# Two layers of an encoder on one core: the output projection as seven block products, and the first gate and up columns together

## The chip, the core and the metric

The kernel runs on one core of a Trainium2 chip. A core has a matrix engine (TensorE, in the profile PE, with its weight loads as PEld), a vector engine (VectorE, DVE), a scalar engine (ScalarE, ACT), GpSimd (POOL), and queues that issue transfers: SP's (SyncE), GpSimd's and ScalarE's. Matrix products land in PSUM, which is used here as eight banks of 512 columns of fp32. Everything else works in SBUF, with 128 partitions. An engine takes its own instructions strictly in the order in which the program wrote them, and waits on semaphores for the others.

The metric is the device time of one execution in microseconds, the median of several runs.

## The reference, cut to what matters

The input is 512 tokens of width 1024, in fp32, and there are two layers. One layer is:

```
h = rms_norm(x, attn_norm_g[l])
z = einsum('bsd,dc->bsc', h, w_in[l])          # q, k, v of two attention branches, and the gates ga, gb
ya = einsum('bsc,cd->bsd', window_gqa(...), w_proj_a[l])
yb = einsum('bsc,cd->bsd', neighbourhood_attn(...), w_proj_b[l])
mixed = sigmoid(ga) * ya + sigmoid(gb) * yb
x = x + einsum('bsd,de->bse', mixed, w_out[l])             # w_out is 1024 x 1024
h = rms_norm(x, ffn_norm_g[l])
u = silu(einsum(h, w_gate[l])) * einsum(h, w_up[l])        # 1024 x 2816 each
x = x + einsum('bsf,fd->bsd', u, w_down[l])                # 2816 x 1024
```

## The kernel before, in words

**Arithmetic.** Activations lie transposed, as eight tiles `xT[k]` of 128 channels by 512 tokens. A product keeps fp32 accuracy by splitting both operands into a high part and the rest: each pair of 128 x 128 weights and 128-row activations costs three matrix products (high by high, high by rest, rest by high). The high part is a ScalarE copy into a rounded type, the rest a VectorE subtraction. For some weights the rest is made another way: ScalarE writes the negated high part and a transfer on GpSimd's queue adds the raw weights to it in SBUF (`low_by_transfer`, `w_low`).

**Seven products.** The feed-forward part (columns 256 and up, in five "quads" of 512 columns) already uses a seven-product scheme: a 2 x 2 split of weights and activations into blocks, seven products of sums of blocks in place of eight. `Quad` loads the four weight blocks and makes their sums and parts; `chain_x` makes the seven activation operands (four sums, seven high parts, seven rests of 128 x 1024 elements each) from the normalised `xn`; `m_step` issues one product, 24 instructions with 256 columns, and evacuates it. The order of the products is `ORDER = (1, 5, 6, 2, 7, 3, 4)`. Four of them share banks. Product 1 goes to bank a; ScalarE copies a into bank b (`seed`). Product 5 goes to bank d and ScalarE fetches it into SBUF. Product 6 adds onto b; VectorE then writes b plus the fetched 5 into a third bank c (`seed_c`, through `plus`). Product 2 adds onto a, product 7 adds onto b, 3 onto c, 4 onto b again.

**The stage of this document.** After the two attention projections (`evac_a`, `evac_b`) come, in each layer:
- the output projection w_out: four column pairs in `pair_matmul`, each 8 x 2 x 3 = 48 products with 512 columns, 192 in all. Each of the eight mixed tiles gets its high part and rest in `chain_m`. `evac_x` adds each result tile to `xT[k]`, and `nrm.chunk` makes the parts of the next norm's operand and the running sum of squares; in layer 0 each tile is also written away to DRAM for later.
- the norm: `Norm.chain` sums the squares over partitions with a tiny product against `ones`, VectorE takes the reciprocal square root of the four columns in 15 tiny instructions, TensorE turns it into rows, VectorE copies the rows to SBUF.
- the first 256 columns of w_gate and then of w_up, as two column pairs (48 products with 512 columns each), `evac_g` and `evac_u`; the norm's row factor is applied only at these evacuations, so that the products may start before the norm is known.
- the quads, which need the normalised `xn`, hence the rows: four scaled VectorE instructions for each half of the channels.
In layer 1, `chain_out` also turns x back to token order with 32 small TensorE products (eight groups of four) and ScalarE copies.

**What sets the order.** The Python code writes one stream of instructions for each engine. A main generator issues the products; side chains (`spawn`) are served in the order of a list and advance when a table of estimated engine times says that their inputs are there (`Need`; with `backlog=XLOG` a chain may run up to 6 us ahead into VectorE's queue). Evacuations (`soon`) and weight preparation (`at_pos`) are tied to positions of the product stream. All buffers lie in two SBUF arenas and eight banks, packed by first and last use. All instructions go through one helper, line 346, so that the profile knows them by tile, operation and shape only.

## Time and profile before

| what | value |
|---|---|
| runs | 1356.54, 1358.61, 1358.91 us; median 1358.61 us |
| the profiled execution | 1358.36 us, of which the span of the profile is 1356.6 us |
| granted clock of TensorE | 1.000 |
| instructions in the span | 21344 |
| ScalarE, GpSimd busy | 844.9 us (62%), 301.5 us (22%) |
| read from and written to HBM | 174.63 MB, 4.19 MB |
| transfers from SBUF to SBUF on GpSimd's queue | 94 |

The profiled execution took 1.8 us more than its span, so a microsecond in the trace is a microsecond of the metric. Page lines give busy time and share; where engines are shown by stage, the columns are the stretch, its length, and for each engine the busy time in it and the number of instructions. Matrix products overlap in the pipeline, so that the mean duration of one is longer than the distance to the next; what counts is the distance from start to start.

### The profile page before, as it was taken

What the parts mean: (1) busy time and instruction counts of PE and PEld (TensorE: products, weight loads), DVE (VectorE), ACT (ScalarE), POOL (GpSimd) and SP (SyncE); (2) the same over time, 40 slices, a digit from 0 to 9 for tenths busy, and PEclk for the clock granted to TensorE, in tenths of its full rate; (3) what the DMA queues carried; (4) which work ended last, traced back from release to release, by engine and by line L of the source; (5) the groups of instructions that cost most, each with busy time, mean ns of one, the idle gap of its engine ahead of it and who ended that gap; (6) DMA issues with size and microseconds to landing.
All of it is one profiled execution on the core that took longest, in us unless ns stands there. A gap on an engine that the chain in (4) does not pass through costs nothing.

```text
span 1356.6 us, 21344 instructions
## 1 busy us (share of the span) xinstructions
PE 1348.2 (99%) x7980; PEld 1195.8 (88%) x7980; DVE 1013.2 (75%) x1856; ACT 844.9 (62%) x1322; POOL 301.5 (22%) x323
## 2 busy tenths in 40 slices
PE   9999999999999999999999999999999999999998
PEld 7888888888899999999888888888888999999997
DVE  6876878455857787878968667784559587878888
ACT  6577677544666657667455676675447656667572
POOL 5542222310211101011243423223002111011110
PEclk9999999999999999999999999999999999999999
DMA  9997888876887778587979978889649867695873
GB/s 224 197 168 137 161 155 150 161 173 202 173 189 188 171 181 202 148 212 192 224 150 197 153 147 149 161 151 185 171 109 168 218 143 171 172 248 123 222 180 98
DMA packets 194279, 234.76 MB, mean 173 GB/s; under 512 B 26992, under 2 KB 156448, under 8 KB 194176
## 3 DMA queue, kind: packets, MB, share of 16 engines
q0 software_dynamic: 102656, 143.64, 56.2%
q1 hardware_dynamic: 91024, 89.08, 22.1%
q8 instruction: 63, 1.03, 0.3%
q10 hardware_dynamic: 496, 0.67, 0.2%
q14 instruction: 40, 0.33, 0.1%
HBM read 174.63 MB, written 4.19 MB: 132 GB/s over the span
## 4 chain that ended last, share of the span: by engine, by line
PE 90%; DVE 4%; ACT 3%; issue 2%; DMA 1%; POOL 0%; SPq 0%; ACTq 0%; POOLq 0%
PE banks L346 90%; DVE arena L346 4%; ACT arena L346 3%; DMA arena<-in_w_in 1%; DMA arena<-in_x 0%; POOL arena L346 0%; ACT sm L346 0%; SPq L346 0%; DVE banks L346 0%; DVE sm L346 0%; DVE den L346 0%; DVE negm L346 0%; ACTq L346 0%; POOLq L346 0%
## 5 line engine op out<-in xcount | busy, mean ns | idle before, releaser
L346 PE MATMUL banks<-arena 128*128 128x512 f32 (+1 forms) x7406 | 1313.6, 337 | 1.6 <-DVE arena L346 0.8
L346 PEld LDWEIGHTS banks<-arena 128*128 128x128 f32 x7406 | 1130.9, 190 | 142.8 <-DVE arena L346 2.2
L346 ACT CAST arena<-arena 128x1024 fp32r<-128x1024 f32 (+2 forms) x377 | 321.2, 882 | 183.8 <-DVE arena L346 172.8
L346 DVE TENSOR_TENSOR arena<-arena,arena 128x1024 fp32r<-128x1024 f32 (+2 forms) x284 | 267.0, 950 | 35.8 <-ACT arena L346 34.0
L346 ACT ACTIVATE arena<-arena 128x1024 fp32r<-128x1024 f32 (+2 forms) x292 | 252.3, 885 | 40.4 <-DMA arena<-in_w_in 19.0
L346 POOL DMA_DIRECT2D arena<-in_w_in x163 | 162.3, 1388 | 313.0 <-ACT arena L346 285.4
L346 DVE TENSOR_TENSOR arena<-arena,banks 128x512 f32<-128x512 f32 (+1 forms) x205 | 138.3, 682 | 121.4 <-PE banks L346 121.3
L346 DVE TENSOR_TENSOR arena<-arena 128x1024 f32<-128x1024 f32 (+4 forms) x256 | 220.7, 875 | 4.5 <-DMA arena<-in_w_gate 2.1
L346 DVE TENSOR_TENSOR arena<-banks,arena 128x512 f32<-128x512 f32 (+4 forms) x230 | 152.8, 669 | 61.4 <-PE banks L346 34.0
L346 POOL DMA_DIRECT2D arena<-arena x94 | 84.2, 896 | 496.7 <-ACT arena L346 335.8
L346 ACT COPY arena<-banks 128x512 f32<-128x512 f32 (+1 forms) x106 | 61.6, 585 | 74.1 <-PE banks L346 72.8
L346 ACT CAST arena<-banks 128x512 fp32r<-128x512 f32 (+2 forms) x116 | 64.4, 555 | 63.8 <-PE banks L346 62.5
L346 ACT ACTIVATE arena<-arena,negm 128x256 f32<-128x256 f32 (+1 forms) x128 | 68.2, 533 | 18.8 <-DVE negm L346 16.9
L346 PE MATMUL banks<-cst,arena 128*128 128x128 f32 x504 | 77.0, 275 | 2.3 <-DMA arena<-in_x 1.0
L346 PEld LDWEIGHTS banks<-cst,arena 128*128 128x128 f32 x504 | 61.6, 141 | 12.3 <-DVE arena L346 1.5
L346 DVE CUSTOM_DVE_ANT_0 arena<-banks,cst,nsnk 128x256 f32<-128x256 f32 (+1 forms) x64 | 34.5, 548 | 33.8 <-PE banks L346 33.1
L346 DVE CUSTOM_DVE_ANT_0 arena<-banks,arena 128x256 f32<-128x256 f32 x64 | 26.4, 420 | 21.5 <-PE banks L346 21.2
L346 ACT ACTIVATE arena<-arena,vec2T 128x512 fp32r<-128x512 f32 x16 | 11.6, 727 | 47.4 <-DVE arena L346 47.4
L346 ACT ACTIVATE arena<-banks 128x512 f32<-128x512 f32 x30 | 18.0, 598 | 35.4 <-PE banks L346 35.3
L346 POOL DMA_DIRECT2D arena<-in_w_up x8 | 8.3, 1035 | 122.7 <-PE banks L346 80.3
L346 DVE TENSOR_SCALAR arena<-arena,sm 128x256 f32<-128x256 f32 (+1 forms) x88 | 29.4, 385 | 1.1
L346 POOL DMA_DIRECT2D arena<-in_w_proj_b x16 | 17.5, 1287 | 52.5 <-ACT arena L346 52.5
(69 smaller groups left out, 366.7 us busy)
## 6 DMA issues: line engine op xcount, KB each, us to landing
arena<-in_w_in POOLq DMA_DIRECT2D x99, 512.0 KB, 7.2
arena<-arena POOLq DMA_DIRECT2D x94, 512.0 KB, 6.8
arena<-in_w_up SPq DMA_DIRECT2D x40, 512.0 KB
arena<-in_w_down SPq DMA_DIRECT2D x40, 512.0 KB
arena<-in_w_gate SPq DMA_DIRECT2D x36, 512.0 KB
arena<-in_w_in POOLq DMA_DIRECT2D x64, 256.0 KB, 6.8
arena<-in_w_proj_a POOLq DMA_DIRECT2D x16, 512.0 KB, 7.4
arena<-in_w_proj_b POOLq DMA_DIRECT2D x16, 512.0 KB, 7.5
```

The source lines that it names most:

```text
L346: f(*args, **kw)
```

## The change

It has four parts.

1. **w_out as two quads.** `plan_out` makes two `Quad`s for each layer, for the output columns 0 to 511 and 512 to 1023, with the loads and sums due 6 and 3 us earlier than the position alone would give. The mixed activations are collected in two tiles `mt` of four channel groups; `chain_seven` (the former `chain_x`, made general, with the high part of operand 5 now made before the rest of operand 1) makes their seven operands. `block_step` (the former `m_step`, made general) issues the products in the order q0: 1, 5; q1: 1, 5; q0: 6, 2, 7, 3, 4; q1: 6, 2, 7, 3, 4. Each finished block is added to a pair of channel tiles `xp` by `add_x`; when both token halves of a pair are there, its two norm chunks are spawned as chains (`gchunk`), and in layer 0 the pair is written away, four transfers of twice the size in place of eight.
2. **Gate and up together.** The first 256 columns of w_gate and w_up use four banks at once: channel tiles 0 to 3 for gate, then for up, then tiles 4 and 5 for all four column tiles, then 6 and 7. Evacuations become chains.
3. **Token order in layer 1.** The change to token-by-column order that layer 1 needs is now made where the gates and projections are evacuated (`into`, `out_of`) and by eight ScalarE copies of x (`chain_turn`) ahead of w_out.
4. **Chain order.** The operands of the first quad go to the head of the list of chains; `chain_out` waits for the up columns to be evacuated; the end of layer 0 (`chain_end`) is put at the head of the list and may run ahead into VectorE's queue.

The core of the diff:

```diff
+    OUT_EARLY = (6.0, 3.0)
...
+    OUT_STEPS = [(q, m) for q in range(2) for m in ORDER[:2]] + [(q, m) for q in range(2) for m in ORDER[2:]]
+
+    def plan_out(l):
+        w = a["w_out"][l]
+        for q in range(2):
+            srcs = [w[512 * h : 512 * h + 512, 512 * q : 512 * q + 512] for h in range(2)]
+            quads[l, q, "w_out"] = Quad(srcs, 0.0, False)
+        for q, m in OUT_STEPS:
+            quads[l, q, "w_out"].due(m, total[0] - OUT_EARLY[q])
+            total[0] += 24 * 0.12
...
     def plan_ffn(l):
-        plan_pair(a["w_gate"][l], 0, KD, on_engines=True)
-        plan_pair(a["w_up"][l], 0, KD)
+        for k0 in range(0, KD, 4):
+            plan_pair(a["w_gate"][l], 0, 4, P * k0, on_engines=True)
+            plan_pair(a["w_up"][l], 0, 4, P * k0)
...
+            yield from begin(0)
+            b11, b12 = tiles[0][:, :, :256], tiles[0][:, :, 256:]
             n1, n2 = buf([4, 256]), buf([4, 256])
-            yield from normal(0)
             yield from high(1, b11)
             V.tensor_tensor(n1, b11, b12, ALU.subtract)
+            yield from high(5, n1)
             yield from low(1)
-            yield from high(5, n1)
             yield from low(5)
-            yield from normal(1)
+            yield from begin(1)
...
+            soon({
+                1: seed,
+                5: fetch,
+                6: seed_c,
+                2: lambda: quadrant(0, 0, o, 1.0),
+                7: lambda: quadrant(1, 1, plus(act()), -1.0),
+                3: lambda: quadrant(0, 1, o, 1.0),
+                4: lambda: quadrant(1, 0, o, -1.0),
+            }[m])
...
+        def add_x(q, i, t, src, sign):
+            at = 2 * q + i
+            x = xp[at][:, :, 256 * t : 256 * t + 256]
+            op = ALU.add if sign > 0 else ALU.subtract
+            V.tensor_tensor(x, x, src.rearrange("p (j n) -> p j n", j=2), op)
+            blocks_of[at] += 1
+            if blocks_of[at] == 2:
+                for j in range(2):
+                    spawn(nrm.gchunk(2 * at + j))
+                if l < DEPTH - 1:
+                    soon(lambda: Q.dma_start(away[at], xp[at]), 1.0)
+
+        for q, m in OUT_STEPS:
+            yield f"m{l}{m}"
+            yield from block_step(quads[l, q, "w_out"], m, ms[m], lambda *x, q=q: add_x(q, *x))
...
+        lead = [mm_bank(), mm_bank(), at_bank(), at_bank()]
+        for k0 in range(0, KD, 4):
+            wk = [w_take(), w_take()]
+            for k1 in range(k0, k0 + 4, 4 if k0 == 0 else 2):
+                for n, o in enumerate(lead):
...
```

How the streams move is seen in three places of layer 0. First TensorE, from the projections to the first quad: the products with 512 columns from the last gates on, the sum of squares against `ones`, the turn of the norm into rows (`rstd`), and the first products with 256 columns of the first quad. Before:

```order
L346 MATMUL banks<-arena_72 128x512 x420
L346 MATMUL banks<-ones,arena_71 128x1 x4
L346 MATMUL banks<-arena_72 128x512 x18
L346 MATMUL banks<-cst,rstd_3112 128x128 x4
L346 MATMUL banks<-arena_72 128x512 x60
L346 MATMUL banks<-arena_72 128x256 x144
```

The same place on TensorE in the change:

```order
L346 MATMUL banks<-arena_72 128x512 x210
L346 MATMUL banks<-arena_72 128x256 x336
L346 MATMUL banks<-arena_72 128x512 x45
L346 MATMUL banks<-ones,arena_71 128x1 x4
L346 MATMUL banks<-arena_72 128x512 x18
L346 MATMUL banks<-cst,rstd_3321 128x128 x4
L346 MATMUL banks<-arena_72 128x512 x33
L346 MATMUL banks<-arena_72 128x256 x144
```

The 192 products of w_out became 336 with half the columns. The product against `ones` stood 18 products behind the end of w_out (the 420 are 210 for what comes before, 192 for w_out and 18 of the 96 for gate and up) and now stands 45 behind it; from the rows to the first quad there were 60 products and there are now 33.

Second VectorE, from the copy of the norm's rows to the second half of the normalised activations (the second `x4`; the 1024-element instruction behind it is the operand of product 6). Before:

```order
L346 COPY arena_71<-banks 128x512
L346 SCALAR_TENSOR_TENSOR arena_71<-arena_71,vec2T 128x512 x4
L346 TENSOR_TENSOR arena_72<-arena_71,arena_72 128x1024
L346 TENSOR_TENSOR arena_71<-banks,arena_71 128x512 x2
L346 TENSOR_TENSOR arena_71<-arena_71 128x1024
L346 TENSOR_TENSOR arena_71<-arena_71 128x4x256
L346 TENSOR_TENSOR arena_72<-arena_71,arena_72 128x1024
L346 TENSOR_TENSOR arena_71<-banks,arena_71 128x512
L346 TENSOR_TENSOR arena_71<-arena_71 128x512
L346 TENSOR_TENSOR arena_72<-arena_71,arena_72 128x1024
L346 SCALAR_TENSOR_TENSOR arena_71<-arena_71,vec2T 128x512 x4
L346 SCALAR_TENSOR_TENSOR arena_71<-arena_71 128x1024
```

The same place on VectorE in the change:

```order
L346 COPY arena_71<-banks 128x512
L346 SCALAR_TENSOR_TENSOR arena_71<-arena_71,vec2T 128x512 x4
L346 TENSOR_TENSOR arena_71<-arena_71 128x1024
L346 TENSOR_TENSOR arena_71<-arena_71 128x4x256
L346 TENSOR_TENSOR arena_72<-arena_71,arena_72 128x1024 x2
L346 SCALAR_TENSOR_TENSOR arena_71<-arena_71,vec2T 128x512 x4
L346 SCALAR_TENSOR_TENSOR arena_71<-arena_71 128x1024
```

The evacuations of gate and up (the rows that read banks) moved out of this stretch to behind it, and the two scaled halves moved together.

Third VectorE, directly behind, up to the instruction that writes a bank from a bank: that is `seed_c`, which reads bank b between products 6 and 7. Before:

```order
L346 SCALAR_TENSOR_TENSOR arena_71<-arena_71 128x1024
L346 TENSOR_TENSOR arena_71<-banks,arena_71 128x512
L346 TENSOR_TENSOR arena_72<-arena_71,arena_72 128x512
L346 TENSOR_TENSOR arena_72<-arena_71,arena_72 128x1024 x2
L346 TENSOR_TENSOR arena_71<-arena_71 128x4x256
L346 TENSOR_TENSOR arena_71<-arena_71 128x512
L346 TENSOR_TENSOR banks<-banks,arena_71 128x512
```

And in the change:

```order
L346 SCALAR_TENSOR_TENSOR arena_71<-arena_71 128x1024
L346 TENSOR_TENSOR arena_71<-banks,arena_71 128x512 x2
L346 TENSOR_TENSOR arena_72<-arena_71,arena_72 128x1024 x2
L346 TENSOR_TENSOR arena_71<-arena_71 128x4x256
L346 TENSOR_TENSOR arena_71<-banks,arena_71 128x512
L346 TENSOR_TENSOR arena_71<-arena_71 128x512
L346 TENSOR_TENSOR arena_72<-arena_71,arena_72 128x1024 x2
L346 SCALAR_TENSOR_TENSOR arena_71<-arena_71 128x1024
L346 TENSOR_TENSOR banks<-banks,arena_71 128x512
```

Between the operand of product 6 and the read of bank b stood six instructions, three of them with 1024 elements, and there now stand ten, six of them with 1024 elements; added are the rests of operands 7 and 3 and the sum for operand 4, and the evacuations of the gate columns. The rest of operand 6 is the first of the first pair.

More of the change, by code (lines that the diff above doesn't have):

```diff
@@ L776, in trunk @@
             plan_pair(a["w_proj_b"][l], 256 * c, 4)
-        for c in range(4):
-            plan_pair(a["w_out"][l], 256 * c, KD, on_engines=True)
+        plan_out(l)
         plan_ffn(l)
@@ L1632, in layer @@
-        last = l == DEPTH - 1
-        A.activation(warm, ones, AF.Silu)
-        spawn(nrm.chain())
-        xo = []
-        def chain_out():
-            yield Need(keys=["x_out", f"rows{nrm.i}"])
-            for b in range(NB):
-                xo.append([act() for _ in range(2)])
-                for half in range(2):
-                    part = xT[4 * half : 4 * half + 4]
-                    yield Need("pe", part, [at_slots])
-                    at_slots.take()
-                    ps = at_bank()
-                    for i in range(4):
-                        T.transpose(ps[:, P * i : P * i + P], part[i][:, P * b : P * b + P], ident)
-                    yield Need("act", [ps])
-                    A.copy(xo[b][half], ps)
-                    at_slots.give(clock["act"])
-            done.add("xo")
@@ L1655, in layer, with chain_seven @@
[L1655 to L1667 removed]
+        def chain_seven(tag, parts, tiles, begin):
@@ new lines, in layer, with chain_out @@
+        for q, m in OUT_STEPS:
+            yield f"m{l}{m}"
+            yield from block_step(quads[l, q, "w_out"], m, ms[m], lambda *x, q=q: add_x(q, *x))
+        last = l == DEPTH - 1
+        A.activation(warm, ones, AF.Silu)
+        spawn(nrm.chain())
+        xo = []
+        def chain_out():
+            yield Need(keys=["x_out", f"rows{nrm.i}", f"{key}up0", f"{key}up1"])
+            for b in range(NB):
+                xo.append([act() for _ in range(2)])
+                for half in range(2):
+                    part = xT[4 * half : 4 * half + 4]
+                    yield Need("pe", part, [end_slots])
+                    end_slots.take()
+                    ps = at_bank()
+                    for i in range(4):
+                        T.transpose(ps[:, P * i : P * i + P], part[i][:, P * b : P * b + P], ident)
+                    yield Need("act", [ps])
+                    A.copy(xo[b][half], ps)
+                    end_slots.give(clock["act"])
+            done.add("xo")
```

281 lines of the change are left out of this document (136 added, 145 removed).

## The prediction

> **What bounds the kernel now.** I read the page's busy times and its chain of waits first.
>
> ```profile
> span 1356.6 us, 21344 instructions
> ...
> PE 1348.2 (99%) x7980; PEld 1195.8 (88%) x7980; DVE 1013.2 (75%) x1856; ACT 844.9 (62%) x1322; POOL 301.5 (22%) x323
> ...
> PE 90%; DVE 4%; ACT 3%; issue 2%; DMA 1%; POOL 0%; SPq 0%; ACTq 0%; POOLq 0%
> ```
>
> TensorE is never idle for long: 1356.6 - 1348.2 = 8.4 us. So a gain has to come from less TensorE time, and a loss from new waits of TensorE. Next comes the view of busy time by stretch: w_out of layer 0, then gate and up, then the first quad's start, the last stretch again in layer 1, and (from a second answer) the gates' end and the projections of layer 1.
>
> ```profile
> core 0: us, PE busy (x) PEld busy (x) DVE busy (x) ACT busy (x) POOL busy (x), PEclk, DMA share, GB/s
> 302.20:345.80 43.60, 43.60 (x194) 36.08 (x194) 24.55 (x32) 18.83 (x25) 2.83 (x3) 1.00 0.62 175
> 345.80:369.00 23.20, 23.20 (x110) 19.30 (x109) 21.17 (x39) 16.48 (x20) 5.97 (x6) 1.00 0.84 181
> 369.00:385.00 16.00, 15.69 (x130) 15.49 (x129) 15.14 (x19) 11.79 (x14) 4.94 (x5) 1.00 1.15 229
> 1039.20:1061.50 22.30, 21.23 (x178) 20.79 (x177) 15.85 (x19) 17.54 (x24) 5.21 (x6) 1.00 1.07 235
> ...
> 925.00:972.50 47.50, 47.50 (x212) 39.30 (x211) 23.73 (x35) 21.97 (x33) 10.95 (x11) 1.00 0.93 204
> ```
>
> In w_out VectorE has 19 us to spare of 43.6; behind it, it is busy for 21.17 of 23.2 (91%) and 15.14 of 16 (95%). Work that is added to VectorE in w_out has room; what it pushes into the next 40 us has none. This is the place to add up.
>
> **What the products save.** The groups of TensorE in two stretches of one shape (94 us of 512 columns, 19 us of 256) give the distance from start to start:
>
> ```profile
> L346 PE MATMUL banks<-arena 128*128 128x512 f32 x416 | 94.5, 389 | 0.0
> ...
> L346 PE MATMUL banks<-arena 128*128 128x256 f32 x160 | 19.4, 283 | 0.0
> ```
>
> (94.5 - 0.389) / 415 = 0.2268 us, and (19.4 - 0.283) / 159 = 0.1202 us. A layer's w_out went through 192 of the first, 43.5 us, and now goes through 336 of the second, 40.4 us: 3.2 us less, 6.4 for both. Gate and up keep their 96 products in another order: nothing. The Trainium skill (TensorE: Matmul & The Clock Gate, Back-to-back issue gap) has N/2.4 + 2.5 ns for a warm isolated product, 215.8 and 109.2 ns; by it the estimate would be 41.4 - 36.7 = 4.7 us per layer and some 3 us more for both. Here the rows differ by 11 and 11 ns from it, and with 1.75 times as many products that costs more than it looks; the rows decide.
>
> **Where TensorE waits now.** TensorE in order of time, first in layer 0, then the two gaps of layer 1:
>
> ```profile
> 349.86 0.95 PE L346 MATMUL banks<-ones,arena 128*128 128x1 f32 x8
> 350.67 4.38 PE L346 MATMUL banks<-arena 128*128 128x512 f32 x18
> 354.89 0.60 PE L346 MATMUL banks<-cst,rstd 128*128 128x128 f32 x4
> 355.25 19.76 PE L346 MATMUL banks<-arena 128*128 128x512 f32 x109
> 375.32 4.94 PE L346 MATMUL banks<-arena 128*128 128x256 f32 x39 [0.31 <-DVE arena L346]
> ```
>
> ```profile
> 1045.55 1.93 PE L346 MATMUL banks<-arena 128*128 128x256 f32 x14 [0.32 <-DVE arena L346]
> ...
> 1051.34 1.09 PE L346 MATMUL banks<-cst,arena 128*128 128x128 f32 x8 [0.76 <-ACT arena L346]
> ```
>
> Between 355.25 and 375.32 stand 60 products of 512 and 49 of 256 columns, 60 x 0.2268 + 49 x 0.1202 = 19.5 us, and 20.07 passed: some 0.5 us of waiting, for the rest of operand 6. Layer 1 waits the same 0.5, and about 1 us for ScalarE when `chain_out` takes its banks.
>
> **VectorE up to the norm.** Its rows in order of time behind w_out of layer 0:
>
> ```profile
> 346.73 0.75 DVE L346 SCALAR_TENSOR_TENSOR arena<-arena,vec2T,arena 128x512 fp32r<-128x512 f32 x1
> 347.40 0.68 DVE L346 TENSOR_TENSOR arena<-arena 128x512 f32<-128x512 f32 x1
> 348.00 0.74 DVE L346 SCALAR_TENSOR_TENSOR arena<-arena,vec2T,arena 128x512 fp32r<-128x512 f32 x1
> ...
> 350.84 0.16 DVE L346 TENSOR_SCALAR sm<-banks 128x4 f32<-128x4 f32 x1 [0.36 <-PE banks L346]
> ...
> 353.62 0.16 DVE L346 SCALAR_TENSOR_TENSOR rstd<-sm,sm 128x4 f32<-128x4 f32 x1
> ...
> 356.09 0.68 DVE L346 COPY arena<-banks 128x512 f32<-128x512 f32 x1
> 356.81 2.74 DVE L346 SCALAR_TENSOR_TENSOR arena<-arena,vec2T 128x512 f32<-128x512 f32 x4
> ...
> 360.60 1.28 DVE L346 TENSOR_TENSOR arena<-banks,arena 128x512 f32<-128x512 f32 x2
> 361.80 2.35 DVE L346 TENSOR_TENSOR arena<-arena 128x1024 f32<-128x1024 f32 x2
> ...
> 368.93 2.73 DVE L346 SCALAR_TENSOR_TENSOR arena<-arena,vec2T 128x512 f32<-128x512 f32 x4
> 371.70 1.23 DVE L346 SCALAR_TENSOR_TENSOR arena<-arena 128x1024 f32<-128x1024 f32 x1
> 372.84 0.69 DVE L346 TENSOR_TENSOR arena<-banks,arena 128x512 f32<-128x512 f32 x1
> ```
>
> From start to start: 0.60 us for 512 elements (347.40 to 348.00), 0.67 scaled (346.73 to 347.40), 1.14 for 1024 (371.70 to 372.84; two take 2.35). Added for each layer are eight sums of weight blocks, eleven instructions for the operands where eight short ones were, and four additions of banks. From the first product of w_out to the last square added, the change's stream has 26 of 1024 elements, 21 of 512 and 8 scaled: 29.6 + 12.6 + 5.4 = 47.6 us. TensorE reaches the `ones` product after 40.4 + 45 x 0.2268 = 50.6 us. So VectorE may stand idle for 3.0 us in all. Walking through its queue, each instruction behind its ScalarE partner, I find 0.2 us at the start, scattered tenths behind casts, and 1.4 us where the last parts wait for ScalarE, which has the table load below before it: 3.4 us, the squares ready at 51.0, TensorE 0.4 us late. Bounds: none at all, or the idle share of the stretch behind w_out, 9% of 52 us, which is 1.7 us late. I take 0.4; the operands of products 6 to 4 come out 1 to 3 us ahead of TensorE in the same walk, and the second block read of bank b 0.1 us late.
>
> ```profile
> 344.61 0.61 ACT L346 ACTIVATE arena<-arena 128x512 f32<-128x512 f32 x1
> ...
> 348.12 1.28 ACT L346 ACT_TABLE_LOAD   x1
> ```
>
> **VectorE from the norm to the first quad.** Count from the `ones` product as zero. It sets VectorE free after 350.84 - 349.86 = 1.0 us, and the 15 tiny instructions end at 353.78 - 349.86 = 3.9, as they do today. TensorE goes on: 18 products and the turn, so that the rows are there at 355.25 - 349.86 = 5.4 and the copy starts at 5.6. Then 33 products remain: the first quad starts at 5.4 + 33 x 0.2268 = 12.9. Today the copy starts 12.9 us ahead of the quad (60 products), then 7.3.
>
> The queue behind the copy, from the order: copy 0.72 (356.09 to 356.81), four scaled 2.77 (368.93 to 371.70), operand 5's difference 1.14, a weight sum 1.14, the rests of 1 and 5 2.28, four scaled 2.77, operand 6's sum 1.14, two evacuations 1.20 (360.60 to 361.80), and the rest of operand 6 1.22: 14.4, so it is there at 20.0. Product 6's second instruction wants it at 12.9 + 5.8 + 0.1 = 18.8. TensorE waits 1.2 us, where it waited 0.5: **+0.7 us**.
>
> The queue goes on: the rest of 2, a sum, an evacuation, a multiplication, the rests of 7 and 3, the sum of 4, and only then the read of bank b: 1.14 + 1.14 + 0.60 + 0.65 + 2.28 + 1.14 + 0.70 = 7.6, at 27.6. Product 6 ends at 20.0 + 23 x 0.12 = 22.8, product 2 at 25.6, and product 7 adds onto the bank that has not been read: **+2.0 us**. Product 3, product 4 and the down columns behind it find what they need in the same walk, so what was late is made good there. Today the read stands at 378.45, waiting for TensorE and not the other way round:
>
> ```profile
> 378.45 0.70 DVE L346 TENSOR_TENSOR banks<-banks,arena 128x512 f32<-128x512 f32 x1 [0.31 <-PE banks L346]
> ```
>
> Bounds of the two together: 0.5 us as today if the queue is not that full, and 5 us if it is another 2 us late.
>
> **What costs nothing.** The six accumulating transfers that each layer gains land in 6.8 us (the page's transfers from SBUF to SBUF) and stand 13 us or more ahead of their product, counted in products; the transfers' share in w_out is 0.62. If that cover were gone, each late one would cost its lateness.
>
> ```profile
> arena<-arena POOLq DMA_DIRECT2D x94, 512.0 KB, 6.8
> ```
>
> The eight ScalarE copies of layer 1, 0.61 us each by the row above, lie under the projections, where ScalarE is busy for 21.97 of 47.5 us (the last stretch above). The four larger transfers away carry the same bytes. Moving `chain_out` behind the up columns still has eight groups for few banks, now the last four in a row: I give it a gain of 0.4 of its 1 us (bounds: 1 less, 1 more). The end of layer 0, where chains move ahead, has 1.2 us of TensorE waits in these rows, so a gain is at most that, and a loss about as much; I take 0.
>
> ```profile
> PEld banks L346 <- ACT arena L346: 0.6, 1, 0.6
> PEld banks L346 <- DVE arena L346: 0.4, 2, 0.3
> ...
> PE banks L346 <- ACT arena L346: 0.2, 1, 0.2
> ```
>
> **The sum.** Layer 0: -3.2 + 0.4 + 0.1 + 0.7 + 2.0 = 0.0. Layer 1 the same, less 0.4. The profiled execution took 1358.36, so 1358.0; the median shown is 0.25 us above it, so 1358.2.
>
> **The rivals.**
> - *Forecast: given back at the first quad.* Of the 3.2 us per layer, 2.0 go to the late read of bank b, and the rest to operand 6 and the norm. 1358.2, own range 1356 to 1361. Chance 0.46.
> - *The saving stays.* The queue drains faster than I add up, so the bank is read in time and operand 6 is as late as today. For it: the same view has VectorE idle again at 378.45, and TensorE never waited for this bank. Against it: my sum between copy and read holds only rows that stand in the stream, and 5.6 us of today's distance are gone. 1358.6 - 6.4 + 2 x 0.5 - 0.4 = 1352.8 (the 0.5 for the norm and bank b in w_out); if only half of it drains, 1355.5. Chance 0.29.
> - *Slower: VectorE falls behind inside w_out.* Each us by which the squares are later than TensorE's 50.6 us is lost in full in each layer, since all behind it counts from there, and the operands of products 6 to 4 have 1 to 3 us. With 2.5 us more idle time between casts and rests than the 3.4 that I walked, it loses 2 x 2.5 us: 1363.2. It decides from 1.4 us per layer beyond my 0.4. For it: 94% of 50.6 us must be busy, and the fullest stretch today reaches 95%. Against it: the stream orders weight work between operands, so there is seldom nothing to do. Chance 0.21.
> - *Cheaper products.* If a product of 256 columns in this stage took half of one of 512, 0.1134 us, w_out would take 38.1 us, 2.3 us less per layer: 1353.6. The distance of 0.1202 holds over all 160 rows, with no reason for another one here: chance 0.02. The Trainium skill's formula (TensorE: Matmul & The Clock Gate, Back-to-back issue gap) points this way.
> - *The change doesn't pay on TensorE at all.* If 256 columns in this stage cost more than 43.5 / 336 = 0.130 us, nothing is saved, and the waits remain: 1358.2 + 6.4 = 1364.6. The quads' 0.1202 speaks against it. Chance 0.02.
>
> **How the numbers follow.** Within 0.2% is 1355.9 to 1361.3, about what runs of this kernel can tell from no change. Of the forecast's 0.46, 0.41 lies there, 0.02 below and 0.03 above; of the second's 0.29, 0.03 lies inside, and of the third's 0.21, 0.03. Faster: 0.02 + 0.26 + 0.02 = 0.30; the same 0.41 + 0.03 + 0.03 = 0.47; slower 0.03 + 0.18 + 0.02 = 0.23. Predicted 1358.2. The range takes in the saving that stays, 1352.8, and the loss of 2.5 us per layer, 1363: from 1352.5 to 1363.5, with some 0.17 outside.
>
> **What would show it.** w_out from the first 256-column product to the first 512-column product: 40.4 us, with no gap over 0.2. The `ones` product 0 to 0.8 us late. In the first quad two gaps of TensorE, about 1.2 us before product 6 and 2.0 before product 7, the second ended by a VectorE instruction on banks; the same in layer 1. VectorE over 90% busy from the end of the projections to product 7. I'm wrong if w_out itself has gaps, if a transfer ends one, or if the two gaps together are under 1 us.

## The result, and the profile after

The changed kernel takes 1365.39 us in the median of five executions (1363.98 to 1369.74), the kernel before 1357.63 (1356.54 to 1358.91): a ratio of 1.0063, 95% interval 1.0044 to 1.0082. Run again beside the first controls it took 1368.05, ratio 1.0082 (1.0067 to 1.0097). So it is slower by 8 to 10 us. The forecast was 1358.2, from 1352.5 to 1363.5; the median lies outside.

The page of the changed kernel, busy times and the chain of waits:

```profile
PE 1345.4 (98%) x8268; PEld 1204.3 (88%) x8268; DVE 1050.6 (77%) x1886; ACT 880.5 (64%) x1360; POOL 311.5 (23%) x335
...
PE 72%; DVE 12%; DMA 6%; ACT 6%; issue 4%; SPq 0%; POOL 0%; ACTq 0%; DVEq 0%; POOLq 0%
```

TensorE is busy 2.8 us less than before, and yet the span is 9.3 us longer (1365.9 against 1356.6). The chain ran through TensorE for 90% of the span; now it is 72%, and other engines and transfers have 28%: TensorE waits. The view of busy time by stretch says where. The rows are, for the changed kernel and then for the kernel before: from w_out's start in layer 0 to the first products of w_down, from there to w_out of layer 1, the same stretch of layer 1, and the rest.

```profile
301.06:387.21 86.15, 82.22 (x589) 77.08 (x588) 78.19 (x103) 59.28 (x72) 16.31 (x16) 1.00 0.82 193
387.21:973.21 586.00, 585.09 (x3519) 520.54 (x3518) 440.85 (x825) 379.15 (x604) 138.86 (x145) 1.00 0.83 179
973.21:1065.17 91.96, 87.14 (x621) 82.00 (x620) 78.33 (x102) 63.31 (x80) 17.53 (x17) 0.98 0.72 156
1065.17:1365.90 300.73, 293.29 (x2013) 272.51 (x2011) 237.02 (x284) 178.22 (x212) 35.15 (x41) 1.00 0.69 172
```

```profile
302.20:386.82 84.62, 84.31 (x446) 72.68 (x445) 62.49 (x88) 47.74 (x59) 13.74 (x13) 1.00 0.79 187
386.82:972.45 585.63, 584.71 (x3518) 520.50 (x3517) 438.00 (x825) 370.77 (x594) 137.29 (x143) 1.00 0.81 177
972.45:1061.48 89.03, 87.96 (x477) 76.12 (x476) 61.51 (x87) 52.89 (x68) 13.04 (x13) 1.00 0.65 150
1061.48:1356.60 295.12, 291.54 (x2012) 272.39 (x2010) 237.44 (x284) 177.88 (x209) 36.30 (x42) 1.00 0.69 171
```

The first number behind the colon pair is the length. The changed stages, where the forecast had a wash, cost 1.5 us more in layer 0 and 2.9 in layer 1; the middle costs 0.4; and the last stretch, whose work the change doesn't touch, costs 5.6 us. (Ahead of w_out the changed execution happens to be 1.1 us early.) TensorE in order of time, the waits in these stages first of layer 0, then of layer 1, then of the last stretch:

```profile
324.52 14.63 PE L346 MATMUL banks<-arena 128*128 128x256 f32 x120 [0.27 <-DVE arena L346]
339.45 13.36 PE L346 MATMUL banks<-arena 128*128 128x256 f32 x69 [0.30 <-DVE arena L346]
353.40 1.05 PE L346 MATMUL banks<-ones,arena 128*128 128x1 f32 x8 [0.59 <-DVE arena L346]
...
373.61 5.90 PE L346 MATMUL banks<-arena 128*128 128x256 f32 x47 [0.88 <-DVE arena L346]
381.38 23.96 PE L346 MATMUL banks<-arena 128*128 128x256 f32 x172 [1.88 <-DVE banks L346]
```

```profile
996.67 14.62 PE L346 MATMUL banks<-arena 128*128 128x256 f32 x120 [0.28 <-DVE arena L346]
1012.49 13.36 PE L346 MATMUL banks<-arena 128*128 128x256 f32 x69 [1.19 <-DVE arena L346]
...
1046.64 5.89 PE L346 MATMUL banks<-arena 128*128 128x256 f32 x47 [0.88 <-DVE arena L346]
1054.41 3.13 PE L346 MATMUL banks<-arena 128*128 128x256 f32 x18 [1.88 <-DVE banks L346]
```

```profile
1162.12 0.50 PE L346 MATMUL banks<-arena 128*128 128x256 f32 x2 [0.31 <-ACT arena L346]
1163.63 12.78 PE L346 MATMUL banks<-arena 128*128 128x256 f32 x88 [1.01 <-DVE arena L346]
1177.06 5.15 PE L346 MATMUL banks<-arena 128*128 128x512 f32 x35 [0.66 <-ACT arena L346]
```

The number in brackets counts from the modelled end of the product before; from start to start, less the product's own 0.1202 or 0.2268 us, the gaps are a little longer, and I give those from here on: in layer 0 0.43, 0.46, 0.75, 1.14 and 2.04 us, in layer 1 0.43, 1.35, 0.75, 1.14 and 2.04. They stand in front of product 4 of w_out's first quad, product 4 of its second quad (w_out's last product), the `ones` product, and products 6 and 7 of the first quad behind. Less the 3.2 us of cheaper products and less 0.5 of old waiting, that is +1.1 in layer 0, to which some restarts of 0.1 us come. In layer 1 a stretch of 3.41 us joins in which the granted clock is 0.5 (half clock; 1.7 us lost, told below), and `chain_out` gives 0.7 back. The three gaps at 1162 to 1177 sum to 2.46, with what stands between them 2.8 us, and a quad later the same comes again with 2.7: that is the 5.6 of the last stretch. The instruction that ends the largest gap, 2.04 us in layer 0, is VectorE's read of bank b, `seed_c`:

```profile
380.54 0.69 DVE L346 TENSOR_TENSOR banks<-banks,arena 128x512 f32<-128x512 f32 x1
```

In front of the first gap of the last stretch, VectorE stood idle, here in the changed kernel and then at the same place before:

```profile
1157.86 1.23 DVE L346 TENSOR_TENSOR arena<-arena 128x1024 f32<-128x1024 f32 x1 [6.69 <-DMA arena<-in_w_gate]
```

```profile
1149.43 1.23 DVE L346 TENSOR_TENSOR arena<-arena 128x1024 f32<-128x1024 f32 x1 [2.05 <-DMA arena<-in_w_gate]
```

A sum of weight blocks waits for the load of a w_gate block, 4.6 us longer than before, and TensorE loses 2.8 of them. SP's queue of these loads, in the changed kernel and before:

```profile
1136.75 6.50 SPq L346 DMA_DIRECT2D arena<-in_w_gate  x3
1144.16 3.50 SPq L346 DMA_DIRECT2D arena<-in_w_down  x2
...
1172.00 0.37 SPq L346 DMA_DIRECT2D arena<-in_w_down  x1
```

```profile
1132.97 3.65 SPq L346 DMA_DIRECT2D arena<-in_w_gate  x3
1139.80 10.30 SPq L346 DMA_DIRECT2D arena<-in_w_down  x2
```

The loads are the same, but go out in another rhythm: three gate loads take 6.5 us to go out instead of 3.65, two down loads follow them in 3.5 us instead of 10.3, and the next down load stands until 1172.0. Before, the second down load went out at 1149.7, when the w_gate block had just landed; in the changed kernel it is under way together with that block. That this is what makes the block late is a reading of these rows and not shown. What the queue itself waits for is mostly VectorE, as the last reader of a load's place; of the waits of SP's queue from 1100 to 1180 in the changed kernel the largest group is

```profile
SPq L346 <- DVE arena L346: 58.1, 8, 19.4
```

So there were four suspects: the order on VectorE in front of product 7, the half clock behind it, something that holds up the end of w_out, and the places of the buffers, which the planner packs anew for each program.

### The profile page after: what moved, and what is told of

Same layout as the page of the kernel before. It is cut to its first block, busy times and chain, and to the rows that moved or that the text cites. A ratio compares the mean times of both kernels' runs of the same rounds, so it can differ in the third digit from the quotient of the medians.

```text
span 1365.9 us, 22021 instructions
## 1 busy us (share of the span) xinstructions
PE 1345.4 (98%) x8268; PEld 1204.3 (88%) x8268; DVE 1050.6 (77%) x1886; ACT 880.5 (64%) x1360; POOL 311.5 (23%) x335
## 4 chain that ended last, share of the span: by engine, by line
PE 72%; DVE 12%; DMA 6%; ACT 6%; issue 4%; SPq 0%; POOL 0%; ACTq 0%; DVEq 0%; POOLq 0%
PE banks L346 72%; DVE arena L346 11%; ACT arena L346 5%; DMA arena<-in_w_gate 4%; DMA arena<-in_w_up 1%; DMA arena<-in_x 1%; ACT L346 0%; SPq L346 0%; DVE banks L346 0%; ACT banks L346 0%; POOL arena L346 0%; ACT warm L346 0%; ACTq L346 0%; DVEq L346 0%; ACT sm L346 0%
## 5 line engine op out<-in xcount | busy, mean ns | idle before, releaser
L346 PE MATMUL banks<-arena 128*128 128x256 f32 (+1 forms) x7694 | 1311.2, 330 | 13.1 <-DVE arena L346 6.1
L346 ACT CAST arena<-arena 128x1024 fp32r<-128x1024 f32 (+2 forms) x387 | 338.4, 903 | 176.8 <-DVE arena L346 158.2
L346 ACT ACTIVATE arena<-arena 128x1024 fp32r<-128x1024 f32 (+2 forms) x304 | 265.3, 892 | 64.5 <-DMA arena<-in_w_in 21.8
L346 DVE TENSOR_TENSOR arena<-arena,arena 128x1024 fp32r<-128x1024 f32 (+2 forms) x282 | 272.6, 978 | 35.4 <-ACT arena L346 33.4
L346 DVE TENSOR_TENSOR arena<-arena 128x1024 f32<-128x1024 f32 (+4 forms) x280 | 247.6, 897 | 22.5 <-DMA arena<-in_w_gate 18.9
L346 POOL DMA_DIRECT2D arena<-arena x106 | 94.2, 888 | 579.7 <-ACT arena L346 347.5
L346 DVE TENSOR_TENSOR arena<-arena,banks 128x512 f32<-128x512 f32 (+1 forms) x201 | 135.3, 681 | 73.7 <-PE banks L346 73.6
L346 DVE SCALAR_TENSOR_TENSOR arena<-arena 128x512 f32<-128x512 f32 (+2 forms) x44 | 32.1, 731 | 0.6
L346 DVE TENSOR_TENSOR banks<-banks,arena 128x512 f32<-128x512 f32 x24 | 16.7, 696 | 18.4 <-PE banks L346 18.4
```

The source lines that it names most:

```text
L346: f(*args, **kw)
```

## The experiments

**The changed kernel again**, as a control.

> The changed kernel itself once more, as a control beside the three below: its five executions spread over 5.8 us (1363.98 to 1369.74 us), those of the kernel before over 2.4. Theory 'its loads arrive on the edge': the spread of 4 to 6 us comes back, VectorE waits 8 to 25 us in all for w_gate blocks, in part in front of other quads than in the first trace (1157.9 and 1219.5 us), while 1.14 and 2.04 us in front of products 6 and 7 and 0.75 us in front of the `ones` product come back within 0.1 us. Rival 'the late blocks are fixed by the program': the same two quads in layer 1 at 2.5 to 3 us each, and nowhere else.

Four executions, 1367.52 to 1371.98 us. In the profiled one VectorE waits 26.9 us for w_gate blocks. The gaps in front of products 6 and 7 come back at 1.14 and 2.04 (2.03 in layer 1), the `ones` product's at 0.75. But w_out's last product waits 0.34 and 1.51 us, the quad at 1164 waits 1.17 and 0.81, the one at 1227 waits 2.18 and 1.17, a gap of 0.26 us in the middle of layer 0 has become 0.35, and a new one of 0.80 stands there. So gaps set by VectorE's order are fixed to 0.02 us, and those that hang on loads wander. The spread came back (4.5 us), and one more quad, in layer 0, waited for its block: that is the first theory, though 26.9 is just over its 8 to 25 us, and the two late quads of layer 1 came back too.

**The read of bank b earlier.**

```diff
-                yield Need("dve", [h], backlog=XLOG)
+                yield Need("dve", [h], backlog=1.0 if tag == "x" and m in (3, 7) else XLOG)
```

> The changed kernel with one rule altered: in the chain that prepares the first quad's operands the rests of operands 7 and 3 may run only 1 us ahead of TensorE's planned clock instead of 6. On VectorE this puts the read of bank b (`seed_c`, 0.70 us) ahead of the rest of operand 3 and of the sum for operand 4 (1.13 us each), behind the rest of 7. Theory 'order on VectorE': product 7's wait, 2.04 us at 381.4 and 1054.4 in the changed kernel's trace, falls by about 2 x 1.13 us to 0 to 0.5 us in both layers, the half clock that followed it in layer 1 (3.41 us at 0.5, so 1.7 us) goes too; 3.5 to 5.5 us less than the changed kernel, and no gap over 0.3 us appears at products 3 and 4. Rival 'VectorE is behind by then, whatever the order': the wait reappears at product 3 or 4 at 1 to 2 us in each layer, and the time stays within 1.5 us of the changed kernel's. Neither theory expects anything of the waits in layer 1's later quads (2.77 and 2.72 us) unless places in the arena move by the way.

1362.75 us in the median of six (1360.23 to 1366.95), 1.0039 (1.0024 to 1.0053). TensorE at the first quad:

```profile
375.12 11.06 PE L346 MATMUL banks<-arena 128*128 128x256 f32 x90 [0.88 <-DVE arena L346]
```

VectorE's read of bank b now stands ahead of two of the 1024-element instructions that it stood behind:

```profile
379.78 0.69 DVE L346 TENSOR_TENSOR banks<-banks,arena 128x512 f32<-128x512 f32 x1
```

Operand 6's wait is the old 1.14, and behind it 90 products run through with no gap over 0.3; so in layer 1. Nothing comes back at products 3 and 4: it is the order on VectorE, as the first theory had it, and worth 2.0 us per layer. The median is 2.6 us below the changed kernel's first one and 5.3 below its second; in the profiled execution other gaps were large, 2.72 us in front of w_out's last product in layer 0 and 1.39 in layer 1, 1.16 and 0.76 in layer 1's later quads, and 0.70, 1.17 and 0.82 in a quad of layer 0.

**TensorE kept busy while it waits.**

```diff
+            if m == 7 and quad.fill:
+                now = clock["pe"]
+                for _ in range(16):
+                    T.matmul(bank["d"][:, :P], idle, idle, start=True, stop=True)
+                clock["pe"] = now
```

> The changed kernel with 16 further 128x128 fp32 products on the constant tile ahead of product 7 of the first quad in both layers, written to bank d, which is read out by then, so that TensorE works while it waits for bank b; their results are thrown away, nothing else is moved. The 16 take 1.7 to 1.9 us at the 0.107 to 0.12 us of a transpose of the same size. Theory 'the clock is lowered by idle time inside one 3.41 us stretch': the stretch at half clock behind product 7 in layer 1 is gone, product 7 starts within 0.4 us of where it started (2.04 us behind its predecessor), the granted clock is 1.0 in every execution where the changed kernel had .997 to 1.0, and the time is 0 to 3.5 us less, 1.7 us in the median. Rival 'the half clock has nothing to do with this gap': it is still there, or the clocks spread from .997 to 1.0 as before, and the time is 0 to 0.5 us more for the added products.

1369.71 us (1364.42 to 1374.01). The filler was too long. The 16 products stand in the trace as 32 instructions, 0.109 us apart:

```profile
379.89 3.74 PE L346 MATMUL banks<-trig 128*128 128x128 f32 x32
383.38 6.93 PE L346 MATMUL banks<-arena 128*128 128x256 f32 x52
```

From start to start that is 3.49 us, where 1.7 to 1.9 were expected and the gap was 2.04. So product 7 started 1.45 us later than without the filler, in both layers, and not within 0.4 us of its place; some 2.9 us of the time are the filler's own. No half clock follows in the profiled execution, but the next run's has none behind the same gap either, and three of six executions still had a mean clock of 0.998 or 0.999 where the theory wanted 1.0 in each. The gaps that hang on loads wandered once more (2.60 us at w_out's last product in layer 1). So the run decides nothing, for the time or for the clock; for the clock the answer came from all traces together, below.

**Other places for the same instructions.** SLACK is the distance in time that the packer tries to keep between two holders of a place. It moves no instruction.

```diff
-SLACK = 4.0
+SLACK = 8.0
```

> The changed kernel with the constant SLACK 8 instead of 4: every engine's instructions and their order stay as they are, only the places of the buffers in the arena and the banks are chosen anew. Theory 'places': the late w_gate blocks in layer 1's later quads (VectorE waits 6.69 us at 1151 and 6.6 us a quad later, TensorE 2.77 and 2.72 us) come from loads that wait for another reader of their place and so run into each other; with new places these waits change by more than 1 us each, and so do the waits of w_out's last products (0.43 and 0.46 us in layer 0, 0.44 and 1.35 us in layer 1), to either side; the time moves by 1 to 6 us, down more likely than up. Rival 'order of the work': the gaps come back within 0.3 us each at the same products, the time within 1.5 us. Neither expects the 1.14 and 2.04 us in front of products 6 and 7 to change by more than 0.2 us, since these are set by VectorE's order.

> The kernel before with SLACK 8 instead of 4, a control for the run above: how much of its time hangs on the places alone. Theory 'places': gaps of 0.5 to 3 us appear at products whose weight blocks are loaded in the second half of the layers, and the time is 1 to 6 us longer, since the kernel before has hardly any gap that could go away (its TensorE chain is 90% of the span). Rival 'order of the work': the same gaps as before within 0.3 us, and the time within 1 us.

The changed kernel with other places: 1363.36 us (1360.14 to 1364.22), 1.0037 (1.0025 to 1.0049). The gaps in the later quads are gone in the profiled execution, none over 0.3 us from 1060 to 1320; VectorE waits 8.2 us for w_gate blocks instead of 18.9. The gaps of 1.14 and 2.04 stayed to 0.01. That speaks for places, against the order of work, in the last stretch; w_out's last product waited 0.59 and 1.74 us, no less than in the changed kernel, so there it is something else. The control fell to the rival: the kernel before takes 1357.76, ratio 1.0001 (0.9992 to 1.0010), with one new gap, of 0.43 us at 739. So a new deal need not cost anything; why the kernel before is less touchy stays open.

**w_up's first block sooner.**

```diff
-            plan_pair(a["w_up"][l], 0, 4, P * k0)
+            plan_pair(a["w_up"][l], 0, 4, P * k0, later_h=-6.0)
```

> The changed kernel with one number altered: the loads of the leading w_up blocks are due 6 us earlier (29 us instead of 23 ahead of their use). The orders of TensorE, VectorE and ScalarE stay; on POOL's queue the first of these loads moves ahead of one accumulating transfer. Theory 'w_up's first block holds ScalarE up inside w_out': ScalarE, in order, waits for this block (or for its place) before it can make the rests, and the norm's chunks, VectorE's additions and the read of bank b queue up behind it, so that the last product of w_out waits (0.46 us in layer 0 and 1.35 in layer 1 in the first trace, 2.72 and 1.39, 0.59 and 2.60, 0.59 and 1.74 in the runs above): this wait falls below 0.3 us in layer 0, and in layer 1 too if it was the load; 0.5 to 3 us less than the changed kernel run beside it. Rival 'VectorE falls behind inside w_out by its own work': the wait stays between 0.4 and 2.7 us and the time does not move.

1362.79 us (1361.55 to 1368.16), against 1368.05 beside it. Both gaps in front of w_out's last product are gone (none over 0.3), and the `ones` product's fell from 0.75 to 0.46. The 5.3 us are more than the 0.5 to 3 that the theory allows: with the longer hold of these loads places were dealt anew, and in this trace the later quads of layer 1 have one gap of 0.82 left. What had happened is seen best in the run with the earlier read of bank b, where this gap was 2.72 us; there ScalarE, then VectorE:

```profile
334.58 1.06 ACT L346 ACTIVATE arena<-arena 128x1024 fp32r<-128x1024 f32 x1 [4.53 <-DMA arena<-in_w_up]
```

```profile
337.23 0.75 DVE L346 SCALAR_TENSOR_TENSOR arena<-arena,vec2T,arena 128x512 fp32r<-128x512 f32 x1 [4.47 <-ACT arena L346]
```

`w_low` makes the negative copy of a w_up block as soon as the planner says, ScalarE waits for the block's load (11.1 us under way), the norm's chunks queue up behind it on ScalarE, VectorE's scaled rests wait for those, and the sum that reads bank b stands behind them on VectorE. The last product of w_out waits for that bank. Running gate and up chunk by chunk had made w_up's first block due 24 products, 5.4 us, sooner. And there is a second reason, on POOL's queue, in layer 0 of the changed kernel and then of this run:

```profile
323.37 0.86 POOL L346 DMA_DIRECT2D arena<-arena  x1 [5.77 <-ACT arena L346]
324.12 0.90 POOL L346 DMA_DIRECT2D arena<-in_w_up  x1
```

```profile
317.55 0.99 POOL L346 DMA_DIRECT2D arena<-in_w_up  x1
323.59 0.84 POOL L346 DMA_DIRECT2D arena<-arena  x1 [5.05 <-ACT arena L346]
```

The load stood behind one of the accumulating transfers that the change added, which itself waits 5.77 us for ScalarE (the kernel before has none in this stage). Due 6 us earlier, it goes ahead of that transfer and out 6.6 us sooner. In layer 1 of the changed kernel the same copy waited for something else, the last TensorE reader of its place:

```profile
1006.09 1.06 ACT L346 ACTIVATE arena<-arena 128x1024 fp32r<-128x1024 f32 x1 [3.20 <-PE banks L346]
```

The run with the earlier load has no such gap either, but with the new places the two effects aren't separated in layer 1.

**Each half of the change alone.** First w_out as seven products, with the old lead:

```diff
+        plan_pair(a["w_gate"][l], 0, KD, on_engines=True)
+        plan_pair(a["w_up"][l], 0, KD)
...
+        for n in range(2):
+            lead = [mm_bank(), mm_bank()] if n == 0 else [at_bank(), at_bank()]
```

> One half of the change alone: the output projection as seven block products as in the changed kernel, but the leading gate products in full ahead of the up products, as in the kernel before, and w_up's two leading blocks needed one after the other behind w_gate's. Theory 'w_up's first block holds ScalarE up': it is needed 5.4 us later, the wait in front of w_out's last product falls below 0.3 us in both layers; but the gate products need the last parts of the norm after 24 products of 0.2268 us instead of 48, and a wait of 1 to 5 us per layer stands in front of them or of the `ones` product. 3 us less to 5 us more than the changed kernel. Rival 'VectorE by its own work': both waits are there, 2 to 10 us more.

1361.78 us (1359.82 to 1363.71), 1.0030 (1.0019 to 1.0041). The wait in front of w_out's last product is gone, and waits of 1.26, 0.47 and 2.37 us (layer 0) and 0.60, 0.47 and 2.36 (layer 1) stand in the lead, the largest for the norm's result:

```profile
359.27 0.65 PE L346 MATMUL banks<-cst,rstd 128*128 128x128 f32 x4 [2.20 <-DVE rstd L346]
```

The waits are those of the first theory; the time is 6.3 us below the changed kernel beside it, where it allowed 3. Layer 1's later quads have no gap here (layer 0's have one of 0.72), and that may be the rest. Then the new lead with the old w_out:

```diff
+        lead = [mm_bank(), mm_bank(), at_bank(), at_bank()]
...
+                        (evac_u if n // 2 else evac_g)(n % 2, o)
```

> The other half of the change alone: the kernel before, its output projection as it was, but with the leading gate and up products run chunk by chunk together, so that w_up's first block is needed 5.4 us sooner. Theory 'w_up's first block holds ScalarE up, and it costs only where VectorE's sums stand behind ScalarE and a bank behind these': in the old projection a bank is read by one addition as soon as its products end, and two further banks are free, so that no gap over 0.3 us appears in front of w_out's products; the time is within 1.5 us of the kernel before. Rival 'the lead costs by itself' (the wait for w_up, the `ones` product's accumulated squares, one row of weights more in the arena): a gap of 0.5 to 3 us per layer in w_out or the lead, or late blocks in the later quads; 1 to 6 us more than the kernel before.

1371.74 us (1369.46 to 1374.03), 13 us more than the kernel before, and neither theory said so much or said why. w_out and lead have no gap, but the first quad starts late in both layers:

```profile
378.39 0.58 PE L346 MATMUL banks<-arena 128*128 128x256 f32 x1 [4.13 <-ACT arena L346]
379.65 12.62 PE L346 MATMUL banks<-arena 128*128 128x256 f32 x85 [0.68 <-DVE arena L346]
```

4.29 and 1.14 us here, 3.01 and 1.14 in layer 1, with three stretches at half clock behind them. This half kept the old rules for who is served first: it evacuates up at once, while the changed kernel spawns the evacuations as chains and lets the operands go first (`first=True`). So it is not quite the change's half; that those rules account for the 4 us was not tried apart.

**All three mended.** The earlier read of bank b, SLACK 8 and the earlier w_up loads.

> The three alterations together: the read of bank b ahead of the rest of operand 3, SLACK 8, and the leading w_up loads 6 us earlier. If the three causes (order on VectorE, places, w_up's first block) are separate and these are all that went wrong: of the changed kernel's trace 4.1 us in front of product 7, 1.7 us of half clock, 5.5 us in the later quads and about 1.5 us in front of w_out's last product are gone, 12 to 13 of 1365.9 us of span, which gives a time of 1354 to 1356 us, 2 to 4 us under the kernel before. If they are not separate (one wait only hands its time to the next): 1358 to 1362 us, no better than the kernel before.

1354.71 us in the median of ten (1352.50 to 1358.43), 0.9980 (0.9970 to 0.9989) of the kernel before: faster than both. That is the time foreseen if the causes are separate. The same four stretches:

```profile
302.15:385.30 83.15, 81.70 (x590) 76.97 (x588) 77.38 (x101) 58.78 (x72) 16.30 (x16) 1.00 0.84 198
385.30:970.89 585.59, 584.87 (x3519) 520.48 (x3518) 441.60 (x825) 379.72 (x605) 138.75 (x145) 1.00 0.83 179
970.89:1057.44 86.55, 85.12 (x621) 80.36 (x620) 78.13 (x102) 62.82 (x80) 17.53 (x17) 1.00 0.77 165
1057.44:1353.80 296.36, 292.26 (x2013) 272.36 (x2011) 237.04 (x284) 178.19 (x212) 35.13 (x41) 1.00 0.70 174
```

The two changed stages now gain 1.5 and 2.5 us on the kernel before; the last stretch still gives 1.2 back.

**The same with SLACK 4 again, with blocks planned sooner, and with SLACK 12.** Three programs with the same instructions on every engine in the same order:

```diff
-SLACK = 8.0
+SLACK = 4.0
```

> The version with all three alterations (1354.71 us in the median), but with SLACK back at 4: the read of bank b ahead of the rest of operand 3 and the earlier w_up loads stay, every engine's instructions and order stay too, only the places are the old choice. Theory 'places make the w_gate blocks late': layer 1's later quads wait again, 1.5 to 6 us in all, VectorE waits 18 to 27 us in all for w_gate blocks instead of 11.5, and the time is 1357 to 1361 us. Rival 'the later quads were late because the stage ahead of them was' (a late start, half clocks, a late w_out): with that stage mended they are in time whatever the places, and the time is within 1.5 us of 1354.7.

```diff
-    LEAD_MOVE, LEAD_LAST, LEAD_SUMS, LEAD_V, LEAD_BLOCK = 7.0, 14.0, 2.0, 20.0, 9.0
+    LEAD_MOVE, LEAD_LAST, LEAD_SUMS, LEAD_V, LEAD_BLOCK = 7.0, 14.0, 2.0, 20.0, 12.0
```

> The version with all three alterations, with the loads of the quads' weight blocks planned 3 us earlier (12 us ahead instead of 9). SP's instructions and their order stay the same, so that all that can change is which place a block gets: one that is free 3 us earlier. Theory 'places': VectorE's 11.5 us of waiting for w_gate blocks fall below 6 and the 0.69 us in front of a product at 1223 goes; 0.3 to 2 us less than 1354.7. Rival 'the transfers themselves are slow there' (three w_gate loads, two w_down loads and POOL's copies share the DMA engines): blocks that go out sooner only run into each other sooner, the waits stay within 3 us of 11.5 and the time within 1 us.

```diff
-SLACK = 8.0
+SLACK = 12.0
```

> The version with all three alterations, with SLACK 12 in place of 8: a further choice of places (636 of 2552 buffers lie elsewhere) for the same instructions in the same order. Choices so far, of the same instructions: 1354.7 (SLACK 8), 1360.5 (SLACK 4), 1361.0 us (SLACK 8, blocks planned 3 us sooner). Theory 'places are a draw': a time anywhere from 1353 to 1362 us, with waits for w_gate blocks or for a place in front of other products than in the other three. Rival 'more distance between two holders of a place is what helped': VectorE's waits for w_gate blocks stay at or below 11.5 us, and the time is at most 1355.5 us.

They take 1360.51 (1356.03 to 1366.25), 1360.97 (1359.05 to 1362.60) and 1355.82 us (1352.59 to 1360.46); ratios 1.0019 (1.0003 to 1.0036), 1.0022 (1.0012 to 1.0031), 0.9986 (0.9973 to 0.9999). VectorE's waits for w_gate blocks (us in all, times, longest) with SLACK 4, 8 and 12:

```profile
DVE arena L346 <- DMA arena<-in_w_gate: 27.6, 6, 6.8
```

```profile
DVE arena L346 <- DMA arena<-in_w_gate: 11.5, 3, 4.8
```

```profile
DVE arena L346 <- DMA arena<-in_w_gate: 17.2, 4, 5.4
```

With SLACK 4 the later quads wait again, although the stages ahead of them are mended: 1.16 and 0.81 us at 1219 and 1232, 1.17 and 0.86 at 1281 and 1295, and the rival of that run falls. (Its places are not quite the changed kernel's, since the w_up loads are held longer.) With blocks planned 3 us sooner no wait of VectorE for a w_gate block is left at all, as the theory of places wants it. But one sum finds another place taken:

```profile
DVE arena L346 <- issue: 7.5, 1, 7.5
```

It starts at 1292.65, just as a transfer of POOL lands (1292.58); TensorE loses 4.2 us there in one gap, with two stretches at half clock behind it, and so both theories of that run miss the time. That POOL's transfer still held the sum's place fits the moment; the view names no releaser, and it wasn't tried apart. SLACK 12 is between: its 17.2 us of waits speak against 'more distance is what helped', and its median is just above that rival's 1355.5. Four programs of the same instructions take 1354.7 to 1361.0 us in the median: places are a draw worth up to 6 us.

## Why the prediction was right or wrong

- **The products.** Right. With its waits mended, w_out takes 40.8 us in both layers (from 302.15 and 970.89 on), 0.4 of it one gap: 336 products at 0.1202.
- **Operand 6, +0.7, and bank b, +2.0.** Right in place, cause and size: 1.14 and 2.04 us where 1.2 and 2.0 were forecast, in both layers, ended by the VectorE instructions named. The earlier read of the bank took away the second and left the first.
- **The `ones` product, +0.4.** Undersized, though inside its bounds of 0 to 1.7: 0.75. 0.3 of it goes with the earlier w_up load.
- **w_out's last product and bank b, +0.1.** The first quad's product 4 waits 0.43, the kind of wait that the term stands for, but four times the size: VectorE reads bank b at 323.69 and has had no idle time since 315. In front of the second quad's product 4 it was wrong: 0.34 to 2.72, as long as w_up's load was not moved. The walk through VectorE's queue let VectorE wait 1.4 us for ScalarE, but ScalarE for no load. The rival 'VectorE falls behind inside w_out', 1363.2, was nearer: VectorE stood idle in front of its rests, as it says, and of the 5 us that it adds 3.2 are in the first trace (2.7 in w_out and 1.5 at `ones`, less the forecast's 1.0). But it names no load, and moving one load took the last product's wait away. The nearest number, 1364.6 of 'the change doesn't pay on TensorE', is luck: its condition, 0.130 us for a product, doesn't hold at 0.1202.
- **"What costs nothing".** This is the step that failed most. It asked whether the added accumulating transfers come late themselves, not what stands behind them on POOL's queue; it left out the load that is moved (w_up's first block, due 5.4 us sooner) and the places, which the packer deals anew to all later loads. The first two stand behind the waits of w_out's last product, in layer 0 at least. And the sum ended at the first quad: that the rest of the program stays as it was holds for its instructions only. In the first trace it took 5.6 us longer, and the same instructions with other places had none of its gaps.
- **The clock.** Not in the sum: a gap of 2.04 us cost 1.7 us more behind it in layer 1, and nothing in layer 0.
- **`chain_out`, -0.4.** Right in sign: its gap of 0.92 us fell to 0.24, part of that at half clock; with all three mended none is left. **The end of layer 0, 0.** +0.4 over the whole middle.
- **"I'm wrong if w_out itself has gaps, if a transfer ends one".** The first came true in the first trace. The second did so one step away: the rows of TensorE's gaps name VectorE and ScalarE, and the transfers stand behind those.

The sum, with what the traces measured: -6.4 for the products, +2.3 for operand 6 and +4.1 for bank b less 1.0 of old waiting, +1.5 for `ones`, +2.7 in w_out, +1.7 half clock, +5.5 later quads, -0.7 `chain_out`: +9.7, against 9.3 between the spans (the sum leaves out the +0.4 of the middle and the 1.1 by which the changed execution reached w_out early).

## What to carry to other kernels

Where a planner gives buffers their places, an edit in one stage redeals the places of all others: before a difference of a few us is put down to the edit, run the same instructions with other places, and put a price on it in the forecast (here up to 6 us on 1355). When two streams are interleaved, look up for each load that is now due sooner who waits for it first, and what stands behind that one in its queue; it was ScalarE here, which nobody would call the bottleneck at 64%. Look too at what a new transfer holds up behind it on its queue. Work that only fills a queue in front of a bank's read can be let wait: one priority was worth 2 us per layer.

## What the runs showed of the hardware

Inside the traces, half clock comes in spells of 3.41 or 6.83 us, on a grid that is fixed within a trace. In layer 1 of the changed kernel, and in layer 0 of the run with the earlier w_up load, the same gap of 2.04 us in front of product 7 (columns as above, the clock is the third number from the end):

```profile
379.86:383.27 3.41, 1.89 (x16) 1.92 (x17) 3.41 (x5) 2.10 (x3) 0.88 (x1) 1.00 1.19 302
1052.29:1055.70 3.41, 1.53 (x14) 1.35 (x13) 3.38 (x6) 3.10 (x4) 0.21 (x1) 1.00 1.06 353
1055.70:1059.12 3.42, 3.42 (x19) 3.42 (x18) 1.69 (x2) 1.01 (x2) 0.69 (x1) 0.50 1.03 234
```

```profile
377.34:380.75 3.41, 1.53 (x14) 1.36 (x13) 3.41 (x5) 3.13 (x4) 0.76 (x1) 1.00 1.18 301
380.75:384.16 3.41, 3.41 (x17) 3.41 (x18) 2.10 (x3) 0.73 (x2) 0.12 (x1) 0.50 1.14 251
...
1053.18:1056.59 3.41, 2.00 (x17) 2.04 (x18) 3.38 (x6) 3.10 (x4) 0.89 (x1) 1.00 1.09 366
```

Where the gap lay inside one stretch of the grid (1.53 of 3.41 us busy), the next stretch ran at half clock, 1.7 us lost; where the grid's border cut it (1.89 and 2.00 busy), nothing followed. Over the traces of all runs, all seven stretches at full clock with at most 1.54 us busy were followed by half clock, and of the seventeen between 1.82 and 2.3 all but two (1.95 and 2.24) were not; so the border is near half of the 3.41, though not sharp by these busy times. Where the grid lies against the program differs between the two traces of the changed kernel, and the clocks differ from execution to execution: the first five of the changed kernel had mean clocks of .999, .999, 1.0, .997 and .999, the one at 1.0 was the fastest (1363.98) and the one at .997 the slowest (1369.74).

The Trainium skill (TensorE: Matmul & The Clock Gate, What's actually happening) describes such a window, 3413 ns long and free-running, and the traces agree: all changes of the clock in a trace are whole multiples of 3.41 us apart. For the loss of the clock it names an idle window, and (HAM oscillation — how this bites in real kernels) idle gaps of over some 3.4 us. Here a gap of 2.04 us was enough, and the measurement decides.
